# Decoder layer on one core: windowed attention with the two kv groups of a block in one unit

## The chip, the cores and the metric

The kernel runs on one core of one Trainium2 chip. The metric is the device time of one execution in microseconds (us). Three runs of the kernel before took 2110.12, 2114.11 and 2117.31 us, so its median is 2114.11 us.

## What is computed

One step of one decoder layer on 1024 prompt tokens and 8 sample tokens (one new token for each of eight running sequences), width 1024: a half-step SwiGLU, a token mixer, a second half-step SwiGLU, and a final norm. The mixer has a sliding-window attention and a gated DeltaNet side by side. The change is in the prompt part of the attention:

```python
def swa_prompt(q, k, v, sinks, slopes):
    # q: (B, T, 2 kv groups, 4 heads each, 64); k, v: (B, T, 2, 64)
    nb = T // WINDOW                      # 8 blocks of 128 queries
    ...                                   # each sees its own and the previous 128 keys
    valid = (dist >= 0) & (dist <= WINDOW) & (blk * WINDOW + c - WINDOW >= 0)
    o = band_attention(qb, band(k), band(v), dist, valid, sinks, slopes)

def band_attention(q, k, v, dist, valid, sinks, slopes):
    s = einsum("...qhgd,...khd->...hgqk", q, k) * (HEAD_DIM ** -0.5)
    s = s - slopes * dist                 # ALiBi
    s = where(valid, s, -inf)
    p = softmax(concatenate([s, sink]))[..., :-1]
    return einsum("...hgqk,...khd->...qhgd", p, v)
```

There are eight query heads. Heads 0 to 3 use kv group 0 and heads 4 to 7 use kv group 1; a head has 64 channels.

## The kernel before

**Stages.** TensorE works through the layer in one order: the first SwiGLU (`ffn_head`, `ffn_in`, `ffn_out`), the mixer's projections (`mix_in`), the mixer's output projection (`mix_out`), the second SwiGLU. Large products are made in three passes of fp32r halves (`mm3`, lines L321 to L323, and `product`, L528 to L530). Attention and DeltaNet use plain fp32 matmuls, which go through `mmul` (L243) and `tr` (L248, transposes). Every instruction of VectorE, ScalarE and GpSimd is recorded under one line, L89, a helper that also books its time; so these are told apart by tile names: `S` are the scores of an attention unit, `aq`, `ak` and `vtok` the queries, keys and values, `nm` and `l` the row minima and row sums, `inv`, `Tb`, `mg`, `conv` belong to the DeltaNet.

**Order of the work.** The order of TensorE's instructions is the order in which the program emits them. The main thread emits the projections. After each group of three matmuls it calls `tick`, which lets background jobs (Python generators) emit their next stage if their time has come. When that is, a small model decides: `mmul` and `tr` advance a planned TensorE time `now`, each VectorE, ScalarE and GpSimd call books a planned duration on its engine, and a job that says `yield PAD_ATT` is called again 1480 ns after its last planned result. The instructions of the other engines are ordered by the framework's scheduler. TensorE waits in order: if the instruction at its head waits for a semaphore, all behind it wait.

**The attention jobs.** The query projection makes two tiles of queries at a time (`q_pair`, called with `j0` = 0 and `j0` = 2). A tile holds one head of each group: head j of group 0 in partitions 0 to 63, and head j + 4, of group 1, in partitions 64 to 127. Keys and values are laid out in the same way. After each `q_pair`, four jobs (`ATT_GENS`) are spawned at once, each with every fourth of 16 units. A unit is one block b of 128 queries and one kv group, and covers two heads:

1. Two score matmuls, one for each head, contract over the 64 partitions of the group (`r`) and write to one PSUM bank. VectorE adds the ALiBi distances while it moves the scores to `S` (SCALAR_TENSOR_TENSOR), and takes the row minimum. ScalarE takes the exponentials and their sums, VectorE the reciprocal, GpSimd scales.
2. Transposes of `S` on TensorE into a second bank, and a ScalarE copy back to SBUF, into the second half of the unit's buffer (`PT`).
3. One or two matmuls with the values, whose output has 64 partitions (again `r`), into a third bank; a ScalarE copy, and a DMA to the scratch tensor `scr` (L964).

Block 0 has 128 keys, the others 256. The units of one `q_pair` are dealt as (block 0, group 0), (block 0, group 1), (block 1, group 0), (block 1, group 1), one to each of the four jobs, and so on.

**Shared resources.** PSUM has eight banks: three in the pool `mm` (projections) and five in the pool `ps`, which attention, DeltaNet, norms and gates share (`pps`). A unit's buffer is one of 44 slots of 1060 columns. The small tiles `nm` and `l` have four buffers each.

The functions that the change touches, and what calls them:

Of the kernel before, what the change touches and what calls it, by code (L numbers as in the profile page):

```python
# [13 lines left out]
AF = mybir.ActivationFunctionType  # L14
ALU = mybir.AluOpType
AX = mybir.AxisListType
# [3 lines left out]
P = 128  # L20
# [3 lines left out]
NB = T // P  # L24
# [19 lines left out]
ATT_GENS = 4  # L44
# [70 lines left out]
class Net:  # L115
# [121 lines left out]
        while any(j in self.bg for j in jobs):  # L237
            self.tick(200.0)

    def mmul(self, out, lhsT, rhs, start=True, stop=True):  # L240
        n = int(np.prod(rhs.shape[1:]))
        self.now += max(110.0, n * 4 / 2.4)
        self.nc.tensor.matmul(out, lhsT, rhs, start=start, stop=stop)  # L243

    def tr(self, out, x):
        p = x.shape[0]
# [674 lines left out]
            self.nc.scalar.copy(vt[:, b0:b0 + 4, :], ps.rearrange("p (b d) -> p b d", b=4))  # L921
            yield -300.0

    def attn_prompt(self, j0, q, k, vt, scr, units):
        nc = self.nc
        for b, kv in units:
            r = slice(kv * 64, kv * 64 + 64)
            nk = P if b == 0 else 2 * P
            k0 = 0 if b == 0 else (b - 1) * P
            h0 = kv * 4 + j0  # L930
            yield from self.need(3)
            buf = self.bt([P, 1026], s="S")
            S = buf[:, :514].rearrange("p (g k) -> p g k", g=2)
            nc.scalar.copy(S[:, :, nk], self.negsink[:, h0:h0 + 2])
            ps = self.pps()
            for g in range(2):
                o = ps[:, g * 256:g * 256 + nk]
                self.mmul(o, q[g][r, b * P:(b + 1) * P], k[r, k0:k0 + nk])
            for g in range(2):
                o = ps[:, g * 256:g * 256 + nk]  # L940
                nc.vector.scalar_tensor_tensor(S[:, g, :nk], self.dist[:, 2 * P - nk:], 2.0 ** -(h0 + g + 1), o, ALU.mult, ALU.subtract)
            nm = self.t("nm", [P, 2], bufs=4)
            nc.vector.tensor_reduce(nm, S[:, :, :nk + 1], AX.X, ALU.min)
            l = self.t("l", [P, 2], bufs=4)
            for g in range(2):
                nc.scalar.activation(S[:, g, :nk + 1], S[:, g, :nk + 1], AF.Exp, bias=nm[:, g:g + 1], scale=-1.0, accum_out=l[:, g:g + 1])
            nc.vector.reciprocal(l, l)
            for g in range(2):
                nc.gpsimd.tensor_scalar(S[:, g, :nk], S[:, g, :nk], l[:, g:g + 1], 1.0, ALU.mult, ALU.mult)
            yield PAD_ATT  # L950
            PT = buf[:, 514:].rearrange("p (a t) -> p a t", a=2)
            nkb = nk // P
            pt = self.pps()
            for kb in range(nkb):
                for g in range(2):
                    self.tr(pt[:, kb * 256 + g * P:kb * 256 + (g + 1) * P], S[:, g, kb * P:(kb + 1) * P])
            nc.scalar.copy(PT[:, :nkb, :], pt[:, :nk * 2].rearrange("p (a t) -> p a t", a=nkb))
# [6 lines left out]
            nc.store.dma_start(scr[r, j0:j0 + 2, b * P:(b + 1) * P], st.rearrange("p (j t) -> p j t", j=2))  # L964
            self.fr(buf)
            yield -300.0

# [438 lines left out]
    def mix_in(self, xhi, xlo, rs, scr, jobs):  # L1406
        nc = self.nc
# [27 lines left out]
        k, v = self.bt(s="ak"), self.bt(s="av")  # L1435
# [323 lines left out]
```

## Time and profile before

| what | value |
|---|---|
| median of the runs | 2114.11 us |
| the profiled execution's own time | 2115.43 us |
| span of its instructions | 2113.2 us |
| TensorE matmul busy | 2024.6 us (96%) |
| VectorE busy | 1222.1 us (58%) |
| ScalarE busy | 699.8 us (33%) |
| GpSimd busy | 594.9 us (28%) |
| mean granted TensorE clock | 0.973 |
| first and last score matmul | 811.3 and 987.4 us |

PE is TensorE (matmul), PEld its weight load, DVE VectorE, ACT ScalarE, POOL GpSimd, SP the queue that issues DMAs. A row of a timeline has the start in us, the duration in us, the engine, the line, the operation, output and inputs, the size of the stationary and of the moving operand, and the number of instructions that were merged into the row. An fp32 matmul of this kernel leaves two records. The end of a matmul in the trace is modelled, and consecutive matmuls overlap in it; the time that a stretch occupies TensorE is therefore best read from its start to the start of what comes next.

### The profile page before, as it was taken

How to read it: one execution, taken by the hardware profiler on the slowest of the kernel's cores; microseconds unless marked ns; L12 is line 12 of the kernel's file. 1: busy time of each engine (PE TensorE's matmuls, PEld its weight loads, DVE VectorE, ACT ScalarE, POOL GpSimd, SP SyncE). 2: the span in 40 equal slices, each digit the busy share in tenths (PEclk: the TensorE clock that was granted, in tenths of full speed). 3: DMA queues.
4: the chain of work that ended last, by engine and by line, in shares of the span. 5: the costliest groups of instructions: out<-in, count | busy, mean ns of one | idle time of the engine just before them, and what ended most of it. 6: DMA issues, size and time to landing. Idle time of an engine off the chain costs nothing.

```text
span 2113.2 us, 37138 instructions
## 1 busy us (share of the span) xinstructions
PE 2024.6 (96%) x15062; PEld 1963.6 (93%) x15062; DVE 1222.1 (58%) x2624; ACT 699.8 (33%) x1491; POOL 594.9 (28%) x517
## 2 busy tenths in 40 slices
PE   7799999999999999999999979999999999999997
PEld 6799999999999998787888869899999999999997
DVE  7755555555533544676977874685555555464335
ACT  5233333333211333545243332443333333331112
POOL 3354444341000131332211111245444444200003
PEclk7999999999999999999999979999999999999999
DMA  4112222227322221211212151221222222552112
GB/s 152 60 58 91 81 73 84 86 71 281 113 68 60 84 81 35 69 45 32 67 46 50 57 181 35 97 70 61 86 81 83 79 81 76 194 195 84 55 41 81
DMA packets 109771, 180.81 MB, mean 86 GB/s; under 512 B 35168, under 2 KB 63744, under 8 KB 109584
## 3 DMA queue, kind: packets, MB, share of 16 engines
q1 hardware_dynamic: 109568, 178.41, 26.6%
q8 instruction: 118, 1.93, 0.4%
q14 instruction: 53, 0.43, 0.1%
q0 software_dynamic: 32, 0.03, 0.0%
HBM read 135.60 MB, written 43.85 MB: 85 GB/s over the span
## 4 chain that ended last, share of the span: by engine, by line
PE 40%; DVE 8%; DMA 1%; issue 1%; SPq 1%; ACT 0%; POOL 0%; DVEq 0%; ACTq 0%; POOLq 0%
PE mm L321 6%; PE mm L322 6%; PE mm L323 6%; PE ps L528 4%; PE ps L530 4%; PE ps L529 4%; PE ps L243 3%; PE mm L528 2%; PE mm L530 2%; PE mm L529 2%; DVE conv L89 1%; DVE inv L89 1%; SPq L102 1%; DVE Tb L89 1%; DVE x L89 1%
## 5 line engine op out<-in xcount | busy, mean ns | idle before, releaser
L528 PE MATMUL ps<-xhi,wop 128*128 128x258 f32 x1480 | 421.0, 284 | 7.4 <-DVE sw L89 7.2
L530 PE MATMUL ps<-xhi,wop 128*128 128x258 f32 x1480 | 419.3, 283 | 0.0
L529 PE MATMUL ps<-xlo,wop 128*128 128x258 f32 x1480 | 419.3, 283 | 0.0
L321 PE MATMUL mm<-hhi,hi 128*128 128x344 f32 x1008 | 322.3, 320 | 0.0
L322 PE MATMUL mm<-hlo,hi 128*128 128x344 f32 x1008 | 322.3, 320 | 0.0
L323 PE MATMUL mm<-hhi,lo 128*128 128x344 f32 x1008 | 321.6, 319 | 0.0
L89 DVE TENSOR_TENSOR wop<-r,wop 128x512 fp32r<-128x512 f32 x185 | 158.5, 859 | 253.9 <-ACT wop L89 239.8
L528 PEld LDWEIGHTS ps<-xhi,wop 128*128 128x128 f32 x1480 | 280.9, 190 | 8.7 <-issue 7.2
L529 PEld LDWEIGHTS ps<-xlo,wop 128*128 128x128 f32 x1480 | 281.9, 191 | 0.0
L530 PEld LDWEIGHTS ps<-xhi,wop 128*128 128x128 f32 x1480 | 281.2, 190 | 0.0
L89 DVE SCALAR_TENSOR_TENSOR x<-mm,x 128x344 f32<-128x344 f32 x240 | 123.3, 515 | 220.0 <-PE mm L323 217.9
L89 ACT CAST hi<-raw 128x1024 fp32r<-128x1024 f32 (+1 forms) x78 | 76.7, 984 | 357.0 <-PE mm L322 327.0
L321 PEld LDWEIGHTS mm<-hhi,hi 128*128 128x128 f32 x1008 | 189.4, 188 | 0.3 <-DVE x L89 0.3
L323 PEld LDWEIGHTS mm<-hhi,lo 128*128 128x128 f32 x1008 | 189.4, 188 | 0.0
L322 PEld LDWEIGHTS mm<-hlo,hi 128*128 128x128 f32 x1008 | 189.3, 188 | 0.0
L89 POOL TENSOR_TENSOR acc<-acc,t 128x344 f32<-128x344 f32 (+1 forms) x50 | 45.5, 911 | 508.2 <-ACT t L89 495.9
L321 PE MATMUL mm<-xnhi,hi 128*128 128x344 f32 x488 | 172.1, 353 | 0.0
L528 PE MATMUL mm<-xhi,wop 128*128 128x258 f32 x592 | 167.5, 283 | 0.0
L530 PE MATMUL mm<-xhi,wop 128*128 128x258 f32 x592 | 167.2, 283 | 0.0
L529 PE MATMUL mm<-xlo,wop 128*128 128x258 f32 x592 | 167.0, 282 | 0.0
L89 ACT CAST wop<-r 128x512 fp32r<-128x512 f32 x185 | 114.7, 621 | 144.6 <-PE mm L530 77.0
L323 PE MATMUL mm<-xnhi,lo 128*128 128x344 f32 x488 | 158.6, 325 | 0.0
(320 smaller groups left out, 4607.5 us busy)
## 6 DMA issues: line engine op xcount, KB each, us to landing
r<-in_w_in SPq DMA_DIRECT2D x86, 512.0 KB, 3.6
hraw<-hd SPq DMA_DIRECT2D x44, 516.0 KB, 5.0
hd<-sw SPq DMA_DIRECT2D x74, 258.0 KB, 2.0
raw<-in_w_out SPq DMA_DIRECT2D x34, 512.0 KB, 4.0
raw<-in_w_mix SPq DMA_DIRECT2D x22, 512.0 KB, 3.6
raw<-in_w_out SPq DMA_DIRECT2D x24, 384.0 KB, 3.2
x<-in_x SPq DMA_DIRECT2D x16, 516.0 KB, 9.0
xd<-x SPq DMA_DIRECT2D x24, 172.0 KB, 1.9
```

The costliest lines, as they stand in the source:

```text
L89: return fn(out, *a, **k)
L102: return self.eng.dma_start(out, src)
L243: self.nc.tensor.matmul(out, lhsT, rhs, start=start, stop=stop)
L321: mm(ps, whi, xhi, start=start, stop=False)
L322: mm(ps, whi, xlo, start=False, stop=False)
L323: mm(ps, wlo, xhi, start=False, stop=stop)
L528: mm(ps, w[:, a], x[0][:, c], start=first, stop=False, skip_group_check=True)
L529: mm(ps, w[:, a], x[1][:, c], start=False, stop=False, skip_group_check=True)
L530: mm(ps, wlo, x[0][:, c], start=False, stop=last, skip_group_check=True)
```

## The change

A unit is now one block with both kv groups: four heads instead of two. The four jobs take blocks 0 to 3, and then 4 to 7. The score matmuls of the two groups alternate (group 0, group 1, group 0, group 1) and go to two banks. The value matmuls alternate as well; both write to one bank, each to its 64 partitions, so that one copy and one DMA bring 128 partitions away. A unit asks for two banks for the scores at once, for two, one after the other, for the transposes, and for one for the output. Both groups' scores lie in one buffer, and the transposed ones are copied back over them. In the planner, the second matmul of a pair advances `now` by 15 ns.

```diff
-    def mmul(self, out, lhsT, rhs, start=True, stop=True):
+    def mmul(self, out, lhsT, rhs, start=True, stop=True, pair=None):
         n = int(np.prod(rhs.shape[1:]))
-        self.now += max(110.0, n * 4 / 2.4)
-        self.nc.tensor.matmul(out, lhsT, rhs, start=start, stop=stop)
+        self.now += 15.0 if pair else max(110.0, n * 4 / 2.4)
+        self.nc.tensor.matmul(out, lhsT, rhs, start=start, stop=stop, skip_group_check=pair is not None)
...
-    def attn_prompt(self, j0, q, k, vt, scr, units):
+    def attn_prompt(self, j0, q, k, vt, scr, blocks):
         nc = self.nc
-        for b, kv in units:
-            r = slice(kv * 64, kv * 64 + 64)
+        R = [slice(kv * 64, kv * 64 + 64) for kv in range(2)]
+        for b in blocks:
...
-            buf = self.bt([P, 1026], s="S")
+            buf = self.bt([P, 1028], s="S")
+            Ss = [buf[:, kv * 514:kv * 514 + 514].rearrange("p (g k) -> p g k", g=2) for kv in range(2)]
...
-            ps = self.pps()
+            ps = [self.pps() for kv in range(2)]
             for g in range(2):
-                o = ps[:, g * 256:g * 256 + nk]
-                self.mmul(o, q[g][r, b * P:(b + 1) * P], k[r, k0:k0 + nk])
+                for kv, r in enumerate(R):
+                    self.mmul(ps[kv][:, g * 256:g * 256 + nk], q[g][r, b * P:(b + 1) * P], k[r, k0:k0 + nk], pair=kv)
+            for kv, S in enumerate(Ss):
+                for g in range(2):
+                    nc.vector.scalar_tensor_tensor(S[:, g, :nk], self.dist[:, 2 * P - nk:], 2.0 ** -(kv * 4 + j0 + g + 1), ps[kv][:, g * 256:g * 256 + nk], ALU.mult, ALU.subtract)
+            for S in Ss:
+                nm = self.t("nm", [P, 2], bufs=4)
...
             yield PAD_ATT
+            PTs = []
+            for kv, S in enumerate(Ss):
+                pt = self.pps()
+                for kb in range(nkb):
+                    for g in range(2):
+                        self.tr(pt[:, kb * 256 + g * P:kb * 256 + (g + 1) * P], S[:, g, kb * P:(kb + 1) * P])
+                PTs.append(buf[:, kv * 514:kv * 514 + 512].rearrange("p (a t) -> p a t", a=2))
+                nc.scalar.copy(PTs[kv][:, :nkb, :], pt[:, :nk * 2].rearrange("p (a t) -> p a t", a=nkb))
             yield PAD_ATT
             po = self.pps()
             for kb in range(nkb):
-                self.mmul(po[r, :256], vt[:, k0 // P + kb, r], PT[:, kb, :], start=kb == 0, stop=kb == nkb - 1)
-            st = buf[r, :256]
-            nc.scalar.copy(st, po[r, :256])
-            nc.store.dma_start(scr[r, j0:j0 + 2, b * P:(b + 1) * P], st.rearrange("p (j t) -> p j t", j=2))
+                for kv, r in enumerate(R):
+                    self.mmul(po[r, :256], vt[:, k0 // P + kb, r], PTs[kv][:, kb, :], start=kb == 0, stop=kb == nkb - 1, pair=kv)
+            st = buf[:, :256]
+            nc.scalar.copy(st, po[:, :256])
+            nc.store.dma_start(scr[:, j0:j0 + 2, b * P:(b + 1) * P], st.rearrange("p (j t) -> p j t", j=2))
...
-            units = [(b, kv) for b in range(NB) for kv in range(2)]
-            return q, [self.spawn(self.attn_prompt(j0, q, k, vt, scr, units[i::ATT_GENS])) for i in range(ATT_GENS)]
+            return q, [self.spawn(self.attn_prompt(j0, q, k, vt, scr, range(i, NB, ATT_GENS))) for i in range(ATT_GENS)]
```

More of the change, by code (lines that the diff above doesn't have):

```diff
@@ L922, in vtok @@
             yield -300.0
[L924 removed]
+    def attn_prompt(self, j0, q, k, vt, scr, blocks):
         nc = self.nc
[L926 to L927 removed]
+        R = [slice(kv * 64, kv * 64 + 64) for kv in range(2)]
+        for b in blocks:
             nk = P if b == 0 else 2 * P
             k0 = 0 if b == 0 else (b - 1) * P
[L930 removed]
+            nkb = nk // P
             yield from self.need(3)
[L932 to L957 removed]
@@ new lines, in attn_prompt @@
+            for kv, S in enumerate(Ss):
[3 more added lines that the diff above has]
+                nm = self.t("nm", [P, 2], bufs=4)
+                nc.vector.tensor_reduce(nm, S[:, :, :nk + 1], AX.X, ALU.min)
+                l = self.t("l", [P, 2], bufs=4)
+                for g in range(2):
+                    nc.scalar.activation(S[:, g, :nk + 1], S[:, g, :nk + 1], AF.Exp, bias=nm[:, g:g + 1], scale=-1.0, accum_out=l[:, g:g + 1])
+                nc.vector.reciprocal(l, l)
+                for g in range(2):
+                    nc.gpsimd.tensor_scalar(S[:, g, :nk], S[:, g, :nk], l[:, g:g + 1], 1.0, ALU.mult, ALU.mult)
@@ new lines, in attn_prompt @@
+            yield PAD_ATT
+            PTs = []
+            for kv, S in enumerate(Ss):
+                pt = self.pps()
+                for kb in range(nkb):
+                    for g in range(2):
+                        self.tr(pt[:, kb * 256 + g * P:kb * 256 + (g + 1) * P], S[:, g, kb * P:(kb + 1) * P])
+                PTs.append(buf[:, kv * 514:kv * 514 + 512].rearrange("p (a t) -> p a t", a=2))
+                nc.scalar.copy(PTs[kv][:, :nkb, :], pt[:, :nk * 2].rearrange("p (a t) -> p a t", a=nkb))
```

1 line of the change is left out of this document (added).

## Prediction

> **What bounds the kernel now.** I read the page first, then a table by stretch, then the timeline of TensorE (PE) around the attention.
>
> ```profile
> span 2113.2 us, 37138 instructions
> PE 2024.6 (96%) x15062; PEld 1963.6 (93%) x15062; DVE 1222.1 (58%) x2624; ACT 699.8 (33%) x1491; POOL 594.9 (28%) x517
> ```
>
> The profiled execution took 2115.43 us, 2.2 more than its span and 1.3 more than the median of the three runs (2114.11). PE is busy nearly all the time, so work taken from PE should shorten the run, unless PE then waits for something else in the same place. The attention runs from 811 to 1000 us; the last head of the DeltaNet ends its projections near 1207.
>
> ```profile
> core 0: us, PE busy (x) PEld busy (x) DVE busy (x) ACT busy (x) POOL busy (x), PEclk, DMA share, GB/s
> 811.00:887.00 76.00, 73.94 (x458) 55.93 (x457) 44.44 (x140) 47.63 (x151) 22.69 (x35) 1.00 0.15 41
> 896.00:1000.00 104.00, 99.89 (x718) 83.18 (x718) 72.06 (x211) 54.04 (x158) 30.32 (x38) 0.97 0.16 39
> ...
> 1200.00:1250.00 50.00, 35.39 (x223) 32.99 (x221) 43.33 (x152) 18.92 (x45) 12.12 (x5) 0.83 0.63 194
> ```
>
> The columns after the length are busy times. In both attention stretches PE is the fullest engine: 2.1 and 4.1 us idle, 6.2 together. In the last row it is not: VectorE (DVE) has 43.33 of 50 us and PE 35.39.
>
> **What attention costs PE, and what a pair costs.** First the value matmuls and the score matmuls of the two attention stretches together, as unions of their busy times (tiles `vtok`, then `aq`):
>
> ```profile
> sum 180.00, PE 26.13 PEld 11.29 ACT 0.00; mean PE 13.06 PEld 5.65 ACT 0.00
> sum 180.00, PE 24.79; mean PE 12.40
> ```
>
> Then single units, four records each (two fp32 matmuls):
>
> ```profile
> 968.32 1.13 PE L243 MATMUL ps<-ak,aq 64*128 64x256 f32 x4
> 969.37 1.08 PE L243 MATMUL ps<-S,vtok 128*64 128x256 f32 x4
> 970.38 0.42 PE L321 MATMUL mm<-xnhi,hi 128*128 128x344 f32 x1
> ```
>
> And places where two units happened to come due together, eight records:
>
> ```profile
> 909.38 0.32 PE L322 MATMUL mm<-xnlo,hi 128*128 128x344 f32 x1
> 909.53 0.32 PE L323 MATMUL mm<-xnhi,lo 128*128 128x344 f32 x1
> 909.78 1.09 PE L243 MATMUL ps<-S,vtok 128*64 128x256 f32 x8
> 910.80 0.43 PE L321 MATMUL mm<-xnhi,hi 128*128 128x344 f32 x1
> ...
> 911.47 1.14 PE L243 MATMUL ps<-ak,aq 64*128 64x256 f32 x8
> 912.54 0.43 PE L321 MATMUL mm<-xnhi,hi 128*128 128x344 f32 x1
> ```
>
> Eight records take 1.14 and 1.09 us where four take 1.13 and 1.08. So two adjacent units of different groups already run side by side, in both stages, and the second is nearly free. Block 0 and the bursts at the spawn show it too; the first row here is block 0's value stage for both groups, the second the first four units' scores:
>
> ```profile
> 833.22 0.65 PE L243 MATMUL ps<-S,vtok 128*64 128x256 f32 x4
> ```
>
> ```profile
> 811.33 1.68 PE L243 MATMUL ps<-ak,aq 64*128 64x128 f32 x16
> 812.94 0.33 PE L866 MATMUL mm<-xnhi,gw 128*16 128x344 f32 x1
> ```
>
> **The change part by part.**
>
> *Matmuls.* There will be 16 pairs, two of them of block 0. Scores: the two bursts' first four units stay at 1.68 each, and 12 pairs cost 1.14: 3.36 + 13.68 = 17.0 against 24.8, a gain of 7.8. Values: 2 × 0.65 + 14 × 1.09 = 16.6 against 26.1, a gain of 9.5. Together 17.3. Bounds: the tables count unions that overlap a neighbour's start by about 0.07, so 15 to 19.
>
> *Entrances.* A stretch of another matmul shape starts 0.25 after the last projection matmul (909.53 to 909.78), where projections follow at 0.15 (909.38 to 909.53). Pairs make 32 entrances of 64 units' stages, so at most 32 × 0.10 = 3.2; many units already share one. I take 1.
>
> *Banks at the spawn.* Four jobs now ask for eight banks of five in one go, where they asked for four. DVE empties them. Its rows after the first spawn:
>
> ```profile
> 812.07 0.49 DVE L89 SCALAR_TENSOR_TENSOR S<-c_dist,ps 128x128 f32<-128x128 f32 x2
> 812.48 2.37 DVE L89 COPY attn_smp<-aq 128x8 f32<-128x8 f32 x1
> 814.76 0.47 DVE L89 SCALAR_TENSOR_TENSOR S<-c_dist,ps 128x128 f32<-128x128 f32 x2
> 815.16 0.74 DVE L89 TENSOR_REDUCE nm<-S 128x2 f32<-128x258 f32 x2
> 815.82 1.07 DVE L89 SCALAR_TENSOR_TENSOR S<-c_dist,ps 128x256 f32<-128x256 f32 x3
> ```
>
> The first two jobs' pairs end at 811.33 + 1.61 = 812.94; the third takes the fifth bank and the first bank again, free at 812.56, and ends near 814.0. The fourth needs the second bank (free at 815.23) and the third, whose two moves are the first two of the last row: about 816.5. PE waits 2.5 us. After the second spawn (scores from 896.40, the same 1.68):
>
> ```profile
> 899.48 0.47 DVE L89 SCALAR_TENSOR_TENSOR S<-c_dist,ps 128x128 f32<-128x128 f32 x2
> ...
> 901.01 0.41 DVE L89 SCALAR_TENSOR_TENSOR S<-c_dist,ps 128x256 f32<-128x256 f32 x1
> ```
>
> The third unit's bank is free at 901.42, the third pair ends at 896.40 + 1.61 + 1.07 = 899.1: 2.3 us. Together 4.8. Bounds: 0, if DVE does all moves first, and 7, if it does every reduce first. Behind the waiting matmul stands all of PE's work: the gates' and the next projection's matmuls, none of which needs a bank of `ps`.
>
> *Clock.* A wait of this size can lower PE's clock (sixth number after the length). PE was idle 1.3 of the four us of the first row and 1.8 of the four of the third:
>
> ```profile
> 924.00:928.00 4.00, 2.70 (x19) 2.40 (x17) 3.84 (x7) 2.17 (x8) 0.00 (x0) 1.00 0.06 23
> 928.00:932.00 4.00, 3.55 (x17) 1.99 (x18) 2.10 (x7) 2.40 (x6) 2.37 (x1) 1.00 0.07 16
> ...
> 976.00:980.00 4.00, 2.23 (x15) 1.36 (x14) 3.90 (x8) 0.42 (x2) 0.94 (x2) 1.00 0.35 128
> 980.00:984.00 4.00, 4.00 (x18) 4.00 (x17) 2.77 (x6) 2.98 (x9) 1.25 (x3) 0.57 0.43 131
> ```
>
> Once the clock stayed at 1.00, once it fell to 0.57 for four us, which is 4 × 0.43 = 1.7 us of work. For two waits I take one such drop, 1.7, between 0 and 3.4. The Trainium skill (TensorE: Matmul & The Clock Gate, section on HAM oscillation) puts the limit at idle gaps of about 3.4 us; by that these waits would cost no clock and the sum would be 1.7 better. The trace does not agree: the 0.57 followed waits that add up to 1.8 us.
>
> *Later stages and the new dealing of the work.* A pair asks for two banks at once, 12 more times for scores and 16 times for transposes; the softmax of its second group starts two DVE moves later; `nm` and `l` have four buffers for up to eight groups in flight; and the planner's shorter PE time puts every later background stage elsewhere between the projections. No row shows these. Bounds from PE's idle time in both stretches now, 6.2 us: gone, or doubled, so −6 to +6. DVE's load there rises from 116.5 of 180 us to 116.5 of about 168, 69%, which leaves room but makes lateness likelier: I take +1.5.
>
> *At no cost.* The output goes out by 16 copies and DMAs instead of 32:
>
> ```profile
> L964 SPq DMA_DIRECT2D scr<-S x32: 574/580/763, 835.3 to 999.8; - x32
> ```
>
> The scratch is read again only after the last projections, near 1210, so size and landing are hidden by 200 us; without that cover each DMA would weigh its issue of 0.58. ScalarE (54.04 of 104) loses 16 copies and is not the bound. Copying the transposed scores back over the scores waits only for the transposes that feed that copy.
>
> *The sum.* −17.3 − 1 + 4.8 + 1.7 + 1.5 = −10.3. 2115.4 − 10.3 = 2105.1 for an execution like the profiled one; 1.3 less for the median, 2104. All terms at their good ends (−19 − 3 + 0 + 0 − 6) would give 2087, all at their bad ends (−15 + 7 + 3.4 + 6) 2117; independent, they make about ±8.
>
> **Rivals.**
>
> *The gain comes back as idle PE.* If the DeltaNet's chain through DVE, not the projections, sets when the mixer ends, PE's gain turns up as longer waits from 1000 to 1250. For it: the row 1200:1250, where PE idles 14.6 us beside a DVE at 87%. Against: the last head's chain starts with projections that PE reaches earlier by all that was gained, and DVE has no more work than before. If only what the last head does not wait for is lost, say three quarters of the 10.3, the time is 2114.1 − 2.6 = 2111.5.
>
> *Waits for banks (slower).* Place: the 28 later two-bank requests. Price: a bank is held until DVE has done what stands ahead of it, typically another group's two moves and its reduce:
>
> ```profile
> L89 DVE SCALAR_TENSOR_TENSOR S<-c_dist,ps 128x256 f32<-128x256 f32 x56 | 21.0, 414 | 5.5 <-PE ps L243 4.8 <-issue 0.6
> L89 DVE TENSOR_REDUCE nm<-S 128x2 f32<-128x514 f32 x28 | 18.8, 677 | 0.2
> ```
>
> That is 2 × 0.41 + 0.68 = 1.5 us. If half the requests wait so long, 14 × 1.5 = 21 us are added to the sum without its last term (−11.8): +9.2, 2123. It decides against the change from 11.8 / 28 = 0.42 us for each request. Against it: per unit no more bank time is used than now, one bank less per pair, and between requests lie several us of projections. The Trainium skill (TensorEngine Tiling (Array Packing), Gotcha 1: PSUM Pressure) states that row tiling raises PSUM pressure, as different row tiles write to different banks; it bears on the scores here, and no run has shown its size yet.
>
> *The pairs do not run side by side.* In the eight-record stretches the groups came one unit after the other, not alternating. If alternation kept them apart, 28 full units would cost 1.13 + 1.08 each and four half ones about half: 28 × 2.21 + 4 × 1.1 = 66 us instead of 50.9, and with the waits (+6.5) 2136. Nothing in the trace speaks for it.
>
> **How the numbers follow.** About 0.3%, 6.3 us, can be told from no change: faster is below 2107.8, slower above 2120.4. The forecast has 0.60 (its own range 2096 to 2112; nine tenths of it below 2107.8), the gain that comes back 0.22, the banks 0.15, the pairs apart 0.03. Faster: 0.54 + 0.03 of the second case = 0.57. Slower: 0.12 of the banks + 0.03 = 0.15. Same: 0.28. The range reaches from 2095 to 2117; above it lie most of the last two cases, below it a few in a hundred.
>
> **What would show it.** Right: score stretches all of eight records at about 1.14 and value stretches of eight at 1.09, their unions near 17 and 16.6 us; a PE wait of 2 to 3 us for DVE `S` in each spawn burst; the first projections after the attention, and the mixer's end, earlier by about 10 us; the same busy time of DVE. Wrong: waits of PE for DVE `S` or ACT `S` at most pairs (the banks); PE idle growth between 1000 and 1250 by as much as the attention gains (the chain); eight records that take over 2 us.

## The result, and the profile after

The changed kernel takes 2127.09 us (median, 2122.92 to 2129.12), the kernel before in the same comparison 2115.71. The ratio is 1.0054, with a 95% interval from 1.0029 to 1.0078: slower by 0.54%, 11.4 us. Forecast were 2104 and a range up to 2117. The profiled execution of the changed kernel took 2126.21 us, 10.8 more than that of before. From its page:

```profile
span 2124.4 us, 37059 instructions
PE 2021.6 (95%) x15062; PEld 1970.1 (93%) x15062; DVE 1230.5 (58%) x2624; ACT 692.6 (33%) x1475; POOL 588.7 (28%) x517
```

PE is busy 3.0 us less than before in a span that is 11.2 us longer, and its mean granted clock is 0.963 instead of 0.973.

**The attention itself became shorter.** The unions of the value and the score matmuls of the changed kernel, from 811 to 1000 us (tiles `vtok`, then `aq`), which stood at 26.13 and 24.79:

```profile
sum 189.00, PE 17.65 PEld 7.78 ACT 0.00; mean PE 17.65 PEld 7.78 ACT 0.00
sum 189.00, PE 19.35 PEld 12.80 DVE 4.10; mean PE 19.35 PEld 12.80 DVE 4.10
```

PE's timeline shows the pairs and what follows them:

```profile
929.48 1.09 PE L243 MATMUL ps<-S,vtok 128*64 128x256 f32 x8
930.50 0.43 PE L321 MATMUL mm<-xnhi,hi 128*128 128x344 f32 x1
...
933.88 1.13 PE L243 MATMUL ps<-ak,aq 64*128 64x256 f32 x8
934.95 0.42 PE L321 MATMUL mm<-xnhi,hi 128*128 128x344 f32 x1
```

Eight records take 1.02 and 1.07 us from their start to the start of the next matmul, as four did. Not all pairs are that short at full clock: the score pair at 853.50 took 1.72 us and the value pair at 864.19 took 1.48. In the first of these the second matmul began 0.66 us after the first, so that only the two in the middle ran side by side; no row shows why.

**The second burst cost more than foreseen.**

```profile
887.54 2.01 PE L243 MATMUL ps<-ak,aq 64*128 64x128 f32 x18
891.27 1.19 PE L243 MATMUL ps<-ak,aq 64*128 64x256 f32 x8 [1.73 <-DVE S L89]
893.29 2.07 PE L243 MATMUL ps<-ak,aq 64*128 64x256 f32 x6 [0.84 <-DVE S L89]
895.29 0.65 PE L321 MATMUL mm<-xnhi,hi 128*128 128x344 f32 x1
```

The brackets give PE's idle time and its releaser: 2.6 us for banks that VectorE empties. What VectorE had in its queue ahead of the moves, with the GpSimd operation beside it:

```profile
888.19 2.34 POOL L89 TENSOR_TENSOR lo<-raw,hi 128x1024 fp32r<-128x1024 f32 x1 [10.68 <-DMA bd<-scr_n]
888.82 1.76 DVE L89 TENSOR_TENSOR inv<-bd,Tb 128x31 f32<-128x31 f32 x1 [0.92 <-DMA bd<-scr_n]
890.74 0.48 DVE L89 SCALAR_TENSOR_TENSOR S<-c_dist,ps 128x128 f32<-128x128 f32 x2
```

An inversion step that takes about 0.2 us elsewhere waited 0.92 us for a DMA and then took 1.76 us; it ended at 890.58, and the GpSimd operation, which had started 0.63 us ahead of it, at 890.53. The first move of the burst came behind it. In stretches of 4 us (length, PE busy, granted clock, DMA share, GB/s):

```profile
888.00:892.00 4.00, 2.27 (x22) 1.00 0.17 16
892.00:896.00 4.00, 3.16 (x12) 0.61 0.31 121
896.00:900.00 4.00, 4.00 (x16) 0.54 0.00 0
900.00:904.00 4.00, 4.00 (x27) 1.00 0.00 0
```

The clock was low in the two rows from 892 to 900. The attention's last value matmul starts at 956.4 us instead of 999.0, and behind it PE was ahead of the kernel before with the projections, but lost more than that afterwards. Starts of projections (in us, from the two traces; k, v and z are the key, value and gate projection of a DeltaNet head, heads counted from 0), and PE's first matmul of the mixer's output projection:

| | k1 | k2 | k3 | z3 | output projection |
|---|---|---|---|---|---|
| before | 944.1 | 1048.7 | 1126.9 | 1211.9 | 1255.06 |
| after | 944.7 | 1031.3 | 1119.5 | 1214.1 | 1272.28 |

Ahead by 17 us at k2, by 7 at k3; behind by 2 at z3 and by 17 at the output projection. From 1270 us on the distance between the two traces stays within 2 us of 12.5.

The lead at k2 is not all time gained. From the first projection of the mixer to k2 (length, PE busy and its records, granted clock, DMA share, GB/s; first before, then after):

```profile
758.38:1048.72 290.34, 280.61 (x1873) 0.98 0.18 51
758.01:1031.32 273.31, 263.82 (x1826) 0.94 0.18 51
```

Both kernels have made the same projections by then and have finished the attention, yet the changed one has 47 records fewer (over the whole run both have 15062): part of the DeltaNet heads' work stands behind k2 that stood ahead of it. The first head's scan (PE's matmuls of `w` and `kd`), for one, starts at 1019.7 instead of 993.5 us, and the third head's at 1199.0 instead of 1173.4. What PE waited for from 1000 to 1310 us, first before, then after (total us, times, longest; the largest groups of the view of waits):

```profile
PE ps L243 <- DVE R L89: 8.2, 7, 2.8
PE ps L243 <- DVE S L89: 5.9, 3, 4.2
PE ps L243 <- DVE qn L89: 4.4, 1, 4.4
PE ps L243 <- ACT w L89: 2.5, 2, 2.1
...
PE ps L248 <- ACT t L89: 1.1, 2, 0.9
```

```profile
PE ps L243 <- ACT w L89: 8.1, 5, 3.5
PE ps L248 <- ACT t L89: 7.8, 3, 4.0
PE ps L243 <- DVE R L89: 7.0, 6, 3.3
PE ps L243 <- DVE qn L89: 6.6, 1, 6.6
PE ps L243 <- DVE S L89: 4.8, 4, 2.2
```

All groups of the view add up to 27 us before and 41 after. Those that grew most are waits for ScalarE (`w`, a scan step's scaled rows; `t`, a head's normalized output). And from the first projection of the mixer to the output projection as a whole, first before, then after:

```profile
758.38:1255.06 496.68, 462.06 (x3198) 0.95 0.23 65
758.01:1272.28 514.27, 464.63 (x3217) 0.91 0.23 64
```

The stretch is 17.6 us longer. PE's idle time grew from 34.6 to 49.6 us, by 15.0, and its busy time by 2.6, although the attention's matmuls take 13.9 us less in it: the granted clock fell from 0.95 to 0.91, and the same work takes longer at a lower clock. So waits and clock together took what the pairs gained, and the loss on top, at about equal parts.

**What such a wait looks like.** VectorE, ScalarE, GpSimd and PE in one timeline of the changed kernel, around the longest one:

```profile
1163.87 0.66 ACT L89 COPY mg<-mg 128x256 f32<-128x256 f32 x1 [4.18 <-DMA mg<-scr_t]
...
1164.56 0.45 DVE L89 STREAM_TRANSPOSE mg<-mg 128x256 f32<-128x256 f32 x1 [2.62 <-ACT mg L89]
...
1174.56 2.71 POOL L89 TENSOR_TENSOR qd<-qd,conv 128x1024 f32<-128x1024 f32 x1 [14.50 <-DVE rsqy L89]
...
1174.99 2.31 DVE L89 TENSOR_TENSOR rsqt<-rsqy 128x16 f32<-128x16 f32 x1
...
1180.84 0.16 DVE L89 SCALAR_TENSOR_TENSOR qn<-smp,rsqy 128x8 f32<-128x8 f32 x1
...
1181.07 3.55 PE L243 MATMUL ps<-kn,st 128*128 128x1 f32 x16 [6.56 <-DVE qn L89]
```

Read it upwards. PE stands still for 6.56 us for `qn`, eight normalized numbers per partition. VectorE reaches it late because its queue is in order: a transpose of the third head's merge stood at its head for 2.62 us, waiting for ScalarE, which waited for a DMA. Behind it VectorE had a backlog: from 1164.5 to 1181.0 us it was busy for 15.87 of 16.5 us. And in that backlog one of the chain's tiny operations took 2.31 us beside a GpSimd operation, and both end at 1177.3 (the other two of its kind took 0.18 and 0.17). Over the whole run VectorE is busy for 58%; here it was short of time, because work had stood in a place where its input was not there yet.

### The profile page after: what moved, and what is told of

It reads as the page before. It is cut to its first block, busy times and chain, and to the rows that moved or that the text cites. A ratio compares the mean times of both kernels' runs of the same rounds, so it can differ in the third digit from the quotient of the medians.

```text
span 2124.4 us, 37059 instructions
## 1 busy us (share of the span) xinstructions
PE 2021.6 (95%) x15062; PEld 1970.1 (93%) x15062; DVE 1230.5 (58%) x2624; ACT 692.6 (33%) x1475; POOL 588.7 (28%) x517
## 4 chain that ended last, share of the span: by engine, by line
PE 45%; DVE 8%; DMA 2%; ACT 1%; issue 1%; SPq 1%; POOL 0%; DVEq 0%; ACTq 0%; POOLq 0%
PE mm L321 7%; PE mm L322 7%; PE mm L323 7%; PE ps L243 5%; PE ps L528 4%; PE ps L530 4%; PE ps L529 4%; PE mm L530 2%; PE mm L528 2%; PE mm L529 2%; DVE conv L89 1%; DVE inv L89 1%; DVE Tb L89 1%; DVE x L89 1%; SPq L102 1%
## 5 line engine op out<-in xcount | busy, mean ns | idle before, releaser
L323 PE MATMUL mm<-hhi,lo 128*128 128x344 f32 x1008 | 322.1, 320 | 0.0
L323 PEld LDWEIGHTS mm<-hhi,lo 128*128 128x128 f32 x1008 | 189.5, 188 | 0.0
L89 POOL TENSOR_TENSOR lo<-raw,hi 128x1024 fp32r<-128x1024 f32 (+1 forms) x30 | 67.3, 2243 | 340.6 <-ACT hi L89 325.4
```

What stands on the lines that cost most here:

```text
L89: return fn(out, *a, **k)
L323: mm(ps, wlo, xhi, start=False, stop=stop)
```

## The experiments

Three theories were on record from the first runs on. **A, dealing:** freed PE time is worth its length, but the planner put the later stages at other places, and that cost the difference. **B, chain:** the DeltaNet's chain through VectorE sets the end of the mixer, and freed PE time comes back as idle time. **C, bursts:** the eight banks that the four jobs ask for at a spawn cost it. Two more came out of the runs: after the first eight **D, fixed queues** (PE's time is set by late results at fixed positions, so work taken out is swallowed by the next wait), and after twelve **E, missing cover** (the projections, the work that hides the DeltaNet heads' latency, run ahead of the heads, and run out first). Ratios are against the kernel before, run beside each on the same chip.

### Is freed TensorE time worth its length?

Kernel before, with half of the attention's score and value matmuls left out, while the planner still books their time:

```diff
             for g in range(2):
-                o = ps[:, g * 256:g * 256 + nk]
-                self.mmul(o, q[g][r, b * P:(b + 1) * P], k[r, k0:k0 + nk])
+                o = ps[:, :nk]
+                if g:
+                    self.now += nk * 4 / 2.4
+                else:
+                    self.mmul(o, q[g][r, b * P:(b + 1) * P], k[r, k0:k0 + nk])
...
             for kb in range(nkb):
-                self.mmul(po[r, :256], vt[:, k0 // P + kb, r], PT[:, kb, :], start=kb == 0, stop=kb == nkb - 1)
+                if kb:
+                    self.now += 256 * 4 / 2.4
+                else:
+                    self.mmul(po[r, :256], vt[:, k0 // P + kb, r], PT[:, kb, :])
```

> The kernel before, with half of the attention's score and value matmuls left out (the second head's scores are read from the first head's, only the first 128 keys meet the values), while the planner still books their time, so that TensorE's order is otherwise that of before. About 25 us less TensorE work in the attention, no new wait for banks. Theory A (dealing: freed TensorE time is worth its length, and the changed kernel lost it because the planner dealt out the background stages at other places): 2115.7 - 20 to 25, about 2093. Theory B (chain: the DeltaNet's chain through VectorE sets the mixer's end, so freed TensorE time comes back as idle): 2108 or more. Theory C (bursts: eight banks asked for at the spawn): as A, since the bursts here ask for four.

Ratio 1.0001 (0.9985 to 1.0016). The unions of the score and value matmuls fell to 14.82 and 16.75 us, 19 us less than before instead of the expected 25, and nothing was gained. The time came back on the spot, in waits and in the clock. PE's waits between 811 and 1000 us, all of the view:

```profile
PE ps L248 <- POOL S L89: 16.8, 9, 4.0
PE ps L243 <- ACT S L89: 0.8, 1, 0.8
PE ps L243 <- DVE NT L89: 0.7, 1, 0.7
```

The kernel before waits 5.5 us there, 12.8 less, and its granted clock from 811 to 1000 us is 0.98, here 0.93. The transposes stand at the places that fit the longer matmuls; now PE reaches them before GpSimd has scaled the scores. With the order kept, A's premise falls; what freed time would be worth in an order made for it, this run doesn't show.

The same for the projections of heads 1 to 3, one pass of three left out:

```diff
-        mm(ps, whi, xlo, start=False, stop=False)
-        mm(ps, wlo, xhi, start=False, stop=stop)
+        light = getattr(self, "light", False)
+        mm(ps, whi, xlo, start=False, stop=stop and light)
+        if not light:
+            mm(ps, wlo, xhi, start=False, stop=stop)
...
+        self.light = True
         for h in range(1, NH):
...
+        self.light = False
```

> The kernel before, with the third pass (L323) left out of the twelve projections of heads 1 to 3 in the mixer, 288 matmuls of about 0.145 us, 42 us of TensorE between 1000 and 1250 us; the order of the rest is the one of before. If TensorE's own work sets the time there: faster by 35 to 42 us, 2070 to 2080. If the jobs' chains set it (fixed queues, late results): TensorE idles in their place, and less than half of it arrives, faster by 0 to 20 us.

Ratio 0.9950 (0.9931 to 0.9969), 10.5 us for 42 us of work. Three quarters went into waits (46 us in all from 1000 to 1310, where the kernel before has 27) and into the clock:

```profile
1000.00:1050.00 50.00, 42.03 (x270) 37.75 (x268) 44.76 (x154) 15.10 (x37) 11.61 (x5) 0.97 0.25 73
1050.00:1100.00 50.00, 39.57 (x317) 35.76 (x316) 40.49 (x129) 21.54 (x60) 7.20 (x3) 0.83 0.22 55
...
1200.00:1250.00 50.00, 35.31 (x171) 30.33 (x169) 37.96 (x116) 19.88 (x44) 10.80 (x5) 0.69 0.61 196
```

The Trainium skill (Perfetto Trace Analysis, Identifying the Most-Contended Engine) says to look for the engine with the highest occupancy, judging TensorE by its MFU (the share of its peak arithmetic) and the busy share of its weight loads and not by that of its matmuls, and to optimize that engine first. By the weight loads, 93% in the row of before, that is PE here too; yet its work was worth nothing in one place and a quarter of its length in another. The measurement decides.

### Is it the DeltaNet's inversion on VectorE?

23 of 31 inversion steps per head left out, booked by the planner, so that PE's order is unchanged:

```diff
         for j in range(31):
             n, w = 31 - j, j // 4 + 1
+            if j >= 8:
+                self.book(nc.vector, 70.0 + 1.04 * n * w, P)
+                self.book(nc.vector, 70.0 + 1.04 * n * w, P)
+                continue
```

In the kernel before, in all heads:

> The kernel before with 23 of the 31 steps of each DeltaNet head's inversion on VectorE left out, while the planner still books them, so that TensorE's order is exactly that of before. It removes no TensorE work. Theory B (the DeltaNet's chain through VectorE sets the mixer's end): faster by 8 to 20 us, 2095 to 2107. Theory A (TensorE's time and the dealing of the stages decide, VectorE only here and there): faster by 0 to 5, 2110 or more.

Ratio 0.9994 (0.9980 to 1.0008). The same in the changed kernel:

> The changed kernel with the same steps left out and TensorE's order exactly that of the changed kernel. B: without the chain the pairs' TensorE gain shows: as fast as the kernel before with the same cut, or up to 12 us faster. A: the loss lies in the dealing and stays: 8 us or more slower than the kernel before with the cut.

Ratio 1.0051 (1.0035 to 1.0067). And in the kernel before, with `if h == 2 and j >= 8`, in the third head only:

> The kernel before with the same steps left out in the third head alone (the head whose last scan step stands just before the mixer's output projection in all traces so far). B: most of the gain of the cut in all heads, 5 to 12 us. A: under 3 us.

Ratio 1.0014 (1.0000 to 1.0028). None gains. B falls in this form: the inversion is not what the mixer ends on, and shortening it doesn't mend the changed kernel.

Both cuts at once in the kernel before, the half matmuls and the short inversions:

> The kernel before with both earlier cuts at once: half of the attention's score and value matmuls (25 us of TensorE) and 23 of the 31 inversion steps of each head (VectorE) are left out, both booked by the planner, so that TensorE's order is the one of before. Each cut alone gave nothing. Theory of alternating limits (TensorE and VectorE limit in turn, so that either cut alone is masked by the other): faster than either alone, by 12 to 30 us. Theory of fixed queues (an instruction at the head of a queue waits for one late result, and everything behind it, whatever its length, waits too): again within 6 us of the kernel before, with the idle time of TensorE between 811 and 1310 us grown by what was left out.

Ratio 0.9965 (0.9948 to 0.9982), 7.4 us. Neither expectation was met: less than the 12 us of alternating limits, more than the nothing that each cut gave alone. There is some masking of one by the other, and most of the work is swallowed all the same.

### Is it the dealing, or the bursts?

Both in the changed kernel. First only the planner's price of a pair is altered:

```diff
-        self.now += 15.0 if pair else max(110.0, n * 4 / 2.4)
+        self.now += max(110.0, n * 4 / 2.4)
```

> The changed kernel, with the second matmul of a pair booked by the planner at its full length (427 ns instead of 15). The chip's work is the same, only the dealing moves. A: the time moves by several us, either way, 2115 to 2135. B: 2127 within 3. C: 2127 within 3, since the spawn still asks for eight banks.

Ratio 1.0059 (1.0038 to 1.0079): no different from the change itself, which all three theories allow. But the order did move: k2 starts at 1045.1 us here and at 1031.3 in the changed kernel, so 14 us of lead there made no difference to the time. Then two jobs instead of four, four banks at a spawn:

```diff
-ATT_GENS = 4
+ATT_GENS = 2
```

> The changed kernel with two attention jobs instead of four, so that a spawn asks for four banks, as before. C: the 4 us wait in the second burst and its lower clock go: 2127 - 5 to 8, about 2120. B: 2127 within 3, the chain is the same. A: moved by several us either way, as every stage is dealt anew.

Ratio 1.0013 (0.9995 to 1.0031), 9 us better than the change. That would fit C. But the kernel before, with the stages of a unit planned farther apart, not an instruction more and no eight-bank burst:

```diff
-PAD_ATT = 1480.0
+PAD_ATT = 1880.0
```

> The kernel before, with the attention stages' waiting margin in the planner at 1880 instead of 1480 ns. The same instructions on every engine, dealt out otherwise. A: moves by over 3 us, up or down. B and C: 2115.7 within 3, as neither the chain nor the bursts change.

Ratio 1.0070 (1.0044 to 1.0097): dealing alone costs as much as the whole change did. Two jobs with `PAD_ATT = 700.0`:

> The changed kernel with two attention jobs and the planner's margin at 700 instead of 1480 ns: the same work, the attention dealt out faster. B: the end of the third head decides, so at best a few us from before: 2108 to 2122. A: a dealing that fits the pairs shows their TensorE gain: 2100 to 2108 if it fits, above 2120 if not.

Ratio 1.0037 (1.0019 to 1.0055), 2119.18 us: in B's range and in neither of A's. The changed kernel with 1880:

> The changed kernel with the attention jobs' planned distance at 1880 ns in place of 1480; the same work and the same requests for eight banks at each spawn. Theory of bursts: those requests cost the 11 us, so this is slower than before too, 2120 to 2130. Theory of dealing: the time moves by some 10 us with any change of the stages' places, in either direction; against the kernel before with the same distance (2129.2) a side by side pair may gain or lose, anywhere from 2105 to 2135.

Ratio 1.0011 (0.9998 to 1.0025), with the same eight-bank requests. PE's timeline of its second burst:

```profile
887.87 2.87 PE L243 MATMUL ps<-ak,aq 64*128 64x128 f32 x26
892.08 1.13 PE L243 MATMUL ps<-ak,aq 64*128 64x256 f32 x6 [1.34 <-DVE S L89]
893.14 0.43 PE L321 MATMUL mm<-xnhi,hi 128*128 128x344 f32 x1
```

5.3 us instead of 7.8, and the clock stayed at 1.00 in the four us after it. What differs is what VectorE had between the moves: here the first four came ahead of the inversion step that had held them up.

```profile
888.61 0.88 DVE L89 SCALAR_TENSOR_TENSOR S<-c_dist,ps 128x128 f32<-128x128 f32 x4 [0.39 <-PE ps L243]
890.11 0.81 DVE L89 TENSOR_TENSOR inv<-bd,Tb 128x31 f32<-128x31 f32 x1 [0.28 <-DMA bd<-scr_n]
```

With 1880 k1 starts 4.6 us earlier than in the changed kernel (940.1) and k2 7.0 us earlier, so much of the gain of 9 us with this distance can be the burst's. The remaining two corners, the kernel before and the changed one with 1080:

> The kernel before with the attention jobs' planned distance at 1080 ns in place of 1480, the other way from the run with 1880, which lost 14.9 us without one instruction more. Theory of dealing: slower than the kernel before as well, by 3 to 15 us, 2115 to 2130, if 1480 lies at a good place by selection; a shorter distance by itself (the chain of an attention unit) would give 2105 to 2113.

> The changed kernel with the attention jobs' planned distance at 1080 ns: the third distance for it, beside 1480 (ratio 1.0054) and 1880 (1.0011), where the kernel before gave 1, 1.0070 at 1880 and 1.0021 at 1080. Theory of dealing: anywhere from 1.000 to 1.008, as the tail of the mixer happens to lie; if its order of the mixer's tail is the same as with 1480, within 4 us of that, 2122 to 2130. Theory of bursts (eight banks asked for at each spawn cost the loss): 1.004 to 1.008 as well.

Ratios 1.0021 (1.0002 to 1.0040) and 1.0051 (1.0032 to 1.0071). In one table:

| planned distance | 1080 | 1480 | 1880 |
|---|---|---|---|
| before | 1.0021 | 1 | 1.0070 |
| after | 1.0051 | 1.0054 | 1.0011 |

By these ratios the change is faster than no change by 0.6% at 1880, and slower by 0.5% at 1480 and by 0.3% at 1080. C as the whole cause falls, for all three changed kernels ask for eight banks at a spawn. As a part of it C stays: the requests cost hardly anything in the first burst, and in the second 2.6 us of waits and a clock of 0.61 and 0.54 over two rows of 4 us. The time moves by 15 us with the dealing alone, more than anything that the change saves.

### Where does the lead go?

With 1880 the changed kernel was ahead of the kernel before by 24 us at k2 (1024.3 against 1048.7), and by 6 at z3; its output projection started at 1265.53, 10 behind. With 1480 it was 17, −2, −17. In the tail of the mixer both have nearly the same order, and both lose over 30 us there. The third head's scan was the suspect, because six of its eight steps lay behind the start of the last projection. Its last three state updates left out, booked by the planner, first in the changed kernel (the same for the other two stages of a step):

```diff
+                skip = h == 2 and c > 4
                 if c == 0:
                     Rr = vr[:, 0, :]
+                elif skip:
+                    self.now += P * 4 / 2.4
+                    self.book(nc.vector, 70.0 + 1.04 * P, P)
+                    yield PAD_SCAN
```

> The changed kernel with the state updates of the last three of eight scan steps left out in the third DeltaNet head alone (nine small matmuls and their nine moves, all booked by the planner; the rest of TensorE's order is unchanged). Theory of the missing cover: in the changed kernel six of these eight steps lie behind the last projection (1226 to 1267 us, 6.9 us a step), where nothing is left for TensorE, and the output projection waits for the slots that this head holds; so the time falls by 12 to 20 us, to 2107 to 2115. Theory that any work taken out of the mixer is swallowed by the next wait: falls by less than 5 us, 2122 or more.

> The same three scan steps of the third head left out of the kernel before, TensorE's order otherwise unchanged. There three steps of this head lie behind the last projection (1223.6 to 1240.2 us, 5.5 us a step), and the output projection starts 13 us after the scan's end. Theory of the missing cover: falls too, by less than the changed kernel, 5 to 14 us, 2100 to 2110; so the gap between the two kernels closes or turns. Theory that it is swallowed: 2109 or more.

Ratios 1.0030 (1.0016 to 1.0043) and 0.9972 (0.9957 to 0.9987). Both gain, 5 and 6 us, so the scan lies on the path; but the changed kernel misses its 12 to 20, and the gap between the two stays. The scan's steps are not what parts them. What is left of E is the cover, not the steps. It can be read as the time from the last projection matmul (L323 on `xnhi`) to the first of the output projection; the changed kernel:

```profile
1233.69 0.32 PE L323 MATMUL mm<-xnhi,lo 128*128 128x344 f32 x1
...
1272.28 0.56 PE L321 MATMUL mm<-mhi,hi 128*128 128x258 f32 x1
```

38.6 us in which PE has only small matmuls of the heads; 24.7 before (1230.35 to 1255.06). The longer stretch is mostly work, not waiting (first before, then after):

```profile
1230.70:1255.06 24.36, 12.08 (x38) 0.55 0.74 207
1234.05:1272.28 38.23, 22.62 (x91) 0.59 0.52 148
```

PE is busy for 10.5 us more, with 91 records instead of 38, at little over half the clock, and idle for 3.3 us more. Four of the third head's eight scan steps are left over for it, where before it was one. So two of the last projections change places in the changed kernel, with their weights' order: the fourth head's values first, which its scan waits for, and the third head's gate, which only the output needs, as cover behind it.

```diff
-            order += [10 + h, 6 + h, 17 + h, 14 + h]
+            order += [10 + h, 6 + h] + ([17 + h, 14 + h] if h < NH - 1 else [14 + h, 17 + h])
...
-            zproj(h - 1)
+            if h < NH - 1:
+                zproj(h - 1)
             d["v"] = self.gdn_conv(8 + h, xhi, xlo)
+            if h == NH - 1:
+                zproj(h - 1)
```

> The changed kernel with the last value projection of the DeltaNet ahead of the third head's gate projection, instead of behind it; the same work, so that the fourth head's chain starts some 25 us earlier and two gate projections lie last. Theory of the missing cover: the last 50 us of projections then stand beside more of the chains, faster than the changed kernel by 5 to 15 us, 2112 to 2122. Theory that the place doesn't matter: 2125 to 2130. If the third head's output, which waits for its gate, becomes late instead: slower than 2130.

Ratio 1.0018 (1.0005 to 1.0030): 7.6 us of the 11.4 are back, and the uncovered stretch shrank from 38.6 to 5.9 us, with no scan step of the third head left for it. That is more than the time gained, since the projections ended 23 us later (1256.5); the output projection started 10 us earlier. The same swap in the kernel before:

> The control for the moved gate projection: the kernel before with the last value projection of the DeltaNet ahead of the third head's gate projection. The changed kernel gained some 7.6 us by this (ratio 1.0054 to 1.0018). If the loss of the changed kernel is one of its own tail order, which the move repairs, the kernel before gains nothing by it: 2108 to 2122. If the move is simply better for both, it gains as much: 2104 to 2109, and the change costs 11 us in either order.

Ratio 1.0002 (0.9986 to 1.0017): nothing to gain there, and the stretch hardly changed (23.4 us). So the swap repairs a loss of the changed kernel's own order. The stretch is not the whole account, though: with the pair booked at its full length it is 23.3 us (1243.05 to 1266.32), as before, and the time no better than the changed kernel's. That order lost more elsewhere: its second burst took 9.2 us, with one wait of 3.22, and the granted clock from 811 to 1000 us was 0.90, against 0.94 in the changed kernel and 0.98 before. Last, swap and distance together in the changed kernel:

> The changed kernel with both alterations that helped it: a planned distance of 1880 ns (ratio 1.0011 by itself, against 1.0054) and the last value projection of the DeltaNet ahead of the third head's gate projection (1.0018 by itself). Its order of TensorE from the mixer's middle on is that of the run with the moved projection. If the two gains lie in different stretches (the one before 1060 us, the other behind 1180), they add: ratio 0.995 to 0.999, 2103 to 2111, the first version with the change that beats the kernel before. If the tail's waits swallow any lead that arrives there: 1.001 to 1.004.

Ratio 0.9979 (0.9962 to 0.9996), 2109.02 us: the first version with the change that beats the kernel before. The two gains add: 1.0054 − 0.0043 − 0.0036 = 0.9975 against 0.9979. Its timeline at the end of the cover:

```profile
1246.12 0.32 PE L323 MATMUL mm<-xnhi,lo 128*128 128x344 f32 x1
...
1251.47 1.25 PE L248 MATMUL ps<-ident,t 128*128 128x128 f32 x4 [5.03 <-ACT t L89]
1252.37 0.56 PE L321 MATMUL mm<-mhi,hi 128*128 128x258 f32 x1
```

6.3 us uncovered, of which 5.03 are one wait for ScalarE.

## Why the prediction was wrong, point by point

- *Matmuls, −17.3:* right in kind, smaller in size. The unions fell by 8.5 (values; 9.5 foreseen) and 5.4 (scores; 7.8 foreseen), 13.9 us. Of the 2.4 that the scores fell short, 1.3 were lost in the second burst, whose last matmuls ran at half clock, and 1.0 in the first stretch (to 887 us), where one pair took 1.70 at a clock of 0.50 (843 to 845 us) and the one at 853.50 took 1.72. The rival that pairs stay apart is refuted.
- *Entrances, −1:* the traces have 24 stretches of attention matmuls where before there were 44. At the prediction's 0.10 each that would be 2 us; no run measures it by itself.
- *Banks at the spawn, +4.8, and clock, +1.7:* right that PE waits for banks that VectorE empties, but the rows were read as VectorE's own pace. The copy of 2.37 us at 812.48 ended with a GpSimd operation that had started at 812.44 (its row is below). In the changed kernel the same copy started at 811.91, ahead of GpSimd, and took 0.17 us; the first burst took 4.06 us with hardly a wait, and its 2.5 were not paid. The rows of the second spawn, too, stood behind a VectorE operation of 1.87 us (897.54) that ended with a GpSimd operation. So the 2.6 us that the second burst waited, for 2.3 foreseen, came near by luck: another operation was held there. The stretches 892 to 900 lost 4 × 0.39 + 4 × 0.46 = 3.4 us of clock, the upper bound.

```profile
812.44 2.38 POOL L89 TENSOR_TENSOR lo<-raw,hi 128x1024 fp32r<-128x1024 f32 x1 [8.93 <-ACT hi L89]
```

- *Waits for banks at most pairs:* one later request waited long, 2.73 us at 924.60, again behind a VectorE operation (2.19 us, from 921.56) that ended with a GpSimd operation. The rival's price of 21 us was not paid; its time, 2123, was near for another reason.
- *No cost of the output's DMAs:* nothing in the traces speaks against it; no wait of PE is put down to them, and the other engines' waits for them fell from 6.6 to 3.2 us.
- *Later stages and the new dealing, +1.5 with bounds −6 to +6:* the step that failed. What the other terms measured (−13.9, +2.6 and at most +3.4) adds up to −7.9, so in an execution that is 10.8 us longer this term came out at some +19. Its bounds came from PE's idle time inside the attention. Dealing works in all of the mixer up to the output projection, where PE's idle time grew by 15 us and the clock fell from 0.95 to 0.91. From one planned distance to another the kernel before moves by 15 us. With bounds of that size the sign of the forecast was open.
- *The range:* 2087 and 2117 were added to the profiled execution's 2115.4; for the median, to which 2104 belongs, they are 1.3 lower. It makes no difference here.
- *The premise beneath:* that time taken from a PE that is 96% busy shortens the run. It holds for a quarter of the projections' work, and not at all for the attention's, with the order kept.
- *The gain comes back as idle PE:* this rival named the right place, 1000 to 1250 us, and the right sign of what happens to the lead. Its price (three quarters of the gain lost) was too small, as more than the gain was lost, and its reason, the chain through VectorE alone, was not borne out where it was tried, at the inversions. The argument against it, that the last head starts earlier by all that was gained, failed: in the changed kernel its key projection started 7 us earlier, its gate projection 2 us later.

What is shown: the attention's matmuls saved 13.9 of the foreseen 17.3 us; waits and a lower clock up to the output projection took that and more; the loss belongs to the order that the planner dealt, since a swap of two projections brings back 7.6 us in this order and nothing in the old one, and another distance of the attention's stages brings back 9, of which 7 stand at k2 already, behind the second burst. What is argued only: that the projections ran out as cover because the changed attention let them pull ahead of the heads. The table of starts, the 47 records that stand behind k2 and the 91 instead of 38 behind the last projection fit it; the scan experiment met half of its number, and the run with the pair booked at full length is as slow without such a tail. Not settled: which of the waits in the tail came first, and why the planner's tail differs in just this way. That the third head stands in line for buffer slots of the first may have part in it; more slots than 44 were not tried.

## What to carry to other kernels

A share of 95% on one engine, read from a program whose queues were laid out with planned distances, does not say that this engine's work is what the time is made of: leave some of it out with the order kept, and see what arrives, before costing a saving at its length. When a change makes the planner deal the later stages anew, take the spread of the time over a few harmless settings of the planner as the uncertainty of the forecast; here 15 us, beside a saving of 14. A row that is long for its size is worth a look at the other engines before its length goes into a sum: here the copy of 2.37 us took 0.17 once it started ahead of GpSimd. And look at what covers the latency at the end of a stage: work that nothing waits for should stand last there.

## What the runs showed of the hardware

- The clock fell with two waits, of 1.73 and 0.84 us, that lay within 4 us (0.61 and 0.54 in the rows from 892 to 900). It did not fall after a single wait of 1.34 us (1.00 in the changed kernel with 1880), nor after one of 2.73 us (1.00 from 924 to 936 in the changed kernel), so the length of the longest wait doesn't tell it. And it can be low beside a busy PE; in the run with two jobs, PE was busy 9.57 of 10 us and got half the clock. No run shows whether its small matmuls or the waits just before that stretch (PE 6.62 of 10 us) did it:

```profile
1030.00:1040.00 10.00, 9.57 (x59) 9.04 (x60) 6.78 (x35) 1.82 (x5) 0.00 (x0) 0.50 0.16 44
```

- Four matmuls that alternate between the two halves of the array's rows, or of its columns, can take the time of two in fp32: 1.07 us for the eight records of a score pair and 1.02 for those of a value pair, where a single unit's four took 1.05 and 1.01 (968.32 to 969.37 to 970.38 in the prediction's rows). Where the second matmul starts late, as at 853.50, they take longer (1.72 us).
- The VectorE operation of 128x16 numbers that took 2.31 us ended with a GpSimd operation that had started 0.43 us ahead of it. The Trainium skill (SBUF — State Buffer, SBUF: two separate sides) says that the two engines share a pair of ports as an exclusive lock, which a VectorE operation with two inputs in SBUF or a GpSimd operation holds for its whole instruction, and that the loser blocks. The rows agree. On a chain of a dozen such tiny operations with PE waiting at its end, this operation took 2.1 us longer than its like; the same happened ahead of both long waits for banks (1.76 and 2.19 us instead of about 0.2).
